# Sums of squares by accumulating transfers, two re-ordered preparation lists, earlier table loads and a pooling split in one streaming-encoder block

## The chip, the cores and the metric

The program runs on one core of one Trainium2 chip. The metric is device time in microseconds (us) of one execution: the median of several executions is what counts. One execution was also recorded by the hardware profiler, and all rows below come from that one. The engines are PE (TensorE, the matrix engine; PEld is its weight load), DVE (VectorE), ACT (ScalarE), POOL (GpSimd) and SP (SyncE, which issues nearly all transfers).

## What is computed

One layer of an encoder block on 1024 tokens of width 1024, in float32:

```python
h = x + 0.5 * swiglu_ffn(rmsnorm(x, norm_ffn1), ffn1_w_in, ffn1_w_out)      # d_ff 2816
u = rmsnorm(h, norm_mix)
q, k, v, g_ret, p, gates = split(u @ w_in)
ret = retention(rotary(q), rotary(k) / 16, v)                 # 4 heads of 256, chunks of 64
ret = ret * rsqrt(mean(ret * ret) + eps) * silu(g_ret)
pool_out = multiscale_pool(p, pool_w, pool_scale)             # windows 2, 4, 8, 16
gate = sigmoid(gates + gate_bias)
merged = gate[0] * (ret @ w_ret_up) + gate[1] * (pool_out @ w_pool_up)
h = h + merged @ w_out
h = h + 0.5 * swiglu_ffn(rmsnorm(h, norm_ffn2), ffn2_w_in, ffn2_w_out)
return rmsnorm(h, norm_final)
```

with `rmsnorm(x, g) = x * rsqrt(mean(x * x) + eps) * g`.

## The kernel before, in words

Every product is made in three matmuls. An operand is split into a high part (a cast on ACT, L164, or a scaled activate, L168) and a low part (the operand less its high part, on DVE, L165 or L169), and PE adds high·high, high·low and low·high (L184, L185, L186). Large products are cut into quarters and done by Strassen's scheme in Winograd's form: seven products in place of eight, whose operands S1 to S4 (of the weights) and T1 to T4 (of the activations) are sums of quarters made on DVE before they are split. The letters behind a tile's name say which product's bank it is (`wo1b` is one of the banks of `wo1`); `c_wS`, `wo1wS`, `vS1w` are weight operands made of such sums, `n3R`, `n3T`, `mgT`, `ruT` activation operands.

The work runs in this order: first feed-forward part (names `a`, norm `n1`), projections and values with their retention and pooling (norm `n2`; `vS`, `q1`, `t1`, `p3`), the merge (`ru` is `w_ret_up`, `wo` is `w_out`, activations `mg`), the second feed-forward part (names `c`, norm `n3`), the final norm. A queue named `flow` holds small steps that are put in by `flow.add` and taken out while products are issued; when a step is put in decides where its instructions stand. A scheduler then sets the order on each engine, in which each engine runs strictly.

A norm works in two stages. While the activations come into being, `Norm.square` squares each block on ACT (L291) and adds it to one tile, here `n3ssq`, on DVE (L303). Later `Next.stats` sums that tile over its partitions on PE (`n3sum`), takes inverse roots on ACT and DVE, and spreads them over the partitions with two matmuls for each half (`n30b`, `n31b`). ACT's functions come in table sets; where another set is needed, an ACT_TABLE_LOAD stands ahead of the function. Two such loads are called for at the program's start by an activate on a one-column tile `warm` (L216 and, in `rotary_tables`, L1190).

`onto` is a transfer issued by POOL that adds its source to its destination; before, it adds the kept residual to the blocks of `wo`. `out_group` makes the blocks of `h` from `w_out`, `handed` puts in the steps that prepare the next product's T operands (its list `f`, by number: 1, 3, 2, 6, 5). `tl`, `raw`, `t4` and `c2` are rings of buffers of their own. In the merge `gates`' tiles (`pg0` to `pg7`) are loaded into `raw`, where the weights of `ru` are loaded too.

Of the kernel before, what the change touches and what calls it, by code (L numbers as in the profile page):

```python
# [13 lines left out]
AF = mybir.ActivationFunctionType  # L14
# [4 lines left out]
S = 1024  # L19
D = 1024  # L20
KT = D // P
# [69 lines left out]
def block_kernel(ctx: ExitStack, tc, x, x_tok, x_two, vecs, f1_in, f1_out, w_in, w_v, pool_w, w_ret, w_pool, w_o,  # L91
# [188 lines left out]
    class Norm:  # L280


        turns = False

        def __init__(self, name):
            self.name, self.ssq, self.seen = name, None, set()
# [6 lines left out]
        def square(self, mt, tokens, src):  # L293
            if self.ssq is None:
                self.ssq = t4(f"{self.name}ssq")
            dst = self.ssq[:, tokens]
            if tokens.start not in self.seen:
                self.squared(dst, src)
                self.seen.update(range(tokens.start, tokens.stop, HD))
            else:  # L300
                q = c2(f"{self.name}q{mt}_{tokens.start}")[:, : tokens.stop - tokens.start]
                self.squared(q, src)
                tt(dst, dst, q, ADD)  # L303

    class Next(Norm):
# [139 lines left out]
                for i in range(4):  # L445
                    flow.add(lambda f=f, i=i: f(i))

        def stats(self, sums=None, between=(), diagonals=None):
            def roots():
                t = sums if sums is not None else token_sums(self.ssq, range(8), self.name)  # L450
                self.r_tok = inverse_root(t, D, self.name)

            def row(q):
                if not q:
                    self.row = t4(f"{self.name}rb")
                to, b = half(self.row, q), spread(self.r_tok[:, 4 * q : 4 * q + 4], f"{self.name}{q}", diagonals)
                if sums is not None:
                    to, b = in_row(to), in_turns(b)
                copy(to, b)
                if q:  # L460
                    self.rb = self.row

            n = max(0, len(between) - 3)
            flow.add(roots, *between[:n], lambda: row(0), *between[n:], lambda: row(1))
# [722 lines left out]
        flow.until(lambda: stored.issuperset(names))  # L1187

    def rotary_tables():
        act(warm, warm, AF.Sigmoid)  # L1190
        for n, z in (("cos", 0), ("sin", 1)):
            tab[n] = t4(n)
            load(tab[n], rope[z])
            tt(tab[n], tab[n], mix.rms(), MUL)

    def project(kind, n):

        at = {"q": 0, "k": KT, "g": 3 * KT, "p": 4 * KT, "t": 5 * KT}[kind] + 2 * n
        name = f"{kind}{n}"
        pair = {}  # L1200
        scaled = kind in "gpt"

        def dest(which):
            tile, j = which
            if tile not in pair:
                pair[tile] = t4(f"{name}{'AB'[tile]}")
            return half(pair[tile], j)

        def evac(which, in0, in1):
            j, dst = which[1], dest(which)  # L1210
            if in1 is not None:
                tt(dst, in0, in1, ADD)
            elif scaled and mix.rb is not None:
                tt(dst, in0, half(mix.rb, j), MUL)
                return
            else:
                copy(dst, in0)
            if scaled and mix.rb is not None:
                tt(dst, dst, half(mix.rb, j), MUL)
            elif scaled:  # L1220
                flow.add(lambda: tt(dst, dst, half(mix.rms(), j), MUL))

        def rotate(j):

            t = {}

            def a():
                if not tab:
                    rotary_tables()
                t["b"], t["c"] = c2(f"{name}b{j}"), c2(f"{name}c{j}")  # L1230
                t["A"], t["B"] = (half(pair[z], j) for z in range(2))
                t["cos"], t["sin"] = half(tab["cos"], j), half(tab["sin"], j)
                tt(t["b"], t["B"], t["sin"], MUL)
                tt(t["c"], t["A"], t["sin"], MUL)

            def b():
                tt(t["A"], t["A"], t["cos"], MUL)
                tt(t["A"], t["A"], t["b"], SUB)

            def c():  # L1240
                tt(t["B"], t["B"], t["cos"], MUL)
                tt(t["B"], t["B"], t["c"], ADD)

            return a, b, c

        def keep(dst):
            for i in range(2):
                load(dst[2 * n + i], pair[i])
            stored.add(name)

        def swish(i):
            act(pair[i], pair[i], AF.Silu)
            load(gs[2 * n + i], pair[i])
            if i:
                stored.add(name)

        def gate(i):
            mt = 2 * n + i
            for j in range(2):
                z = c2(f"{name}z{i}{j}")  # L1260
                act(in_row(z), in_turns(half(pair[i], j)), AF.Sigmoid, bias=vec[:, V_B0 + mt : V_B0 + mt + 1])
                load(half(gates[mt], j), z)
            if i:
                stored.add(name)

        def window(i):

            win = 2 << n
            t = {}

            def double(step):
                s = t.get("s", pair[i])
                o = t["s"] = t4(f"{name}s{i}_{step}")
                tt(o[:, step:], s[:, step:], s[:, : S - step], ADD)
                copy(o[:, :step], s[:, :step])

            def mean():
                z, s = pair[i], t["s"]

                edge = sb.tile([P, 16], F32, tag="edge", bufs=2, name=f"{name}e{i}")  # L1280
                tt(edge, s[:, :16], cst[:, C_CNT + 16 * n : C_CNT + 16 * n + 16], MUL)
                tt(edge, edge, z[:, :16], SUB)
                stt(s, s, 1.0 / win, z, MUL, SUB)
                copy(s[:, :16], edge)
                load(pooled[2 * n + i], s)
                if i:
                    stored.add(name)

            return *(lambda b=b: double(1 << b) for b in range(n + 1)), mean

        def end():
            if kind in "qk":
                turn = (*rotate(0), *rotate(1)) if n < NH - 1 or kind == "k" else ()
                flow.add(*turn, lambda: keep(qs if kind == "q" else ks))
            elif kind == "p":
                flow.add(*window(0), *window(1))
            else:
                f = swish if kind == "g" else gate
                flow.add(lambda: f(0), lambda: f(1))

        return lambda shared: strassen(mix, w_in[at], w_in[at + 1], name, evac, end, shared=shared, dest=dest)

    def values():
# [70 lines left out]
        def result(o, j, other=None):  # L1374
            def after(i, b):
                c = c2(f"vc{o}{j}{i}")
                if other is None:
                    copy(c, b)
                else:
                    tt(c, b, other(i), ADD)  # L1380
                flow.add(lambda: store(o, j, i, c))
                if (o, j, i) == (0, 0, 3):
                    nx.stats(between=nx.blocks("R22", [("tl", N_TL)] * 3, True))

            return after

# [14 lines left out]
        s2, s1 = product("S2", "T2", "a", False, after6), product("S1", "T1", "b", True, after5)  # L1401
        nx.work(nx.t3)
        for k in range(4):
            if k == 2:
                nx.work(nx.r21, nx.t4_)
            yield (lambda a=s2[k], b=s1[k]: (a[0](), b[0]())), s1[k][1]
            yield (lambda: None), s2[k][1]
        for p in zip(product("S4", "R22", "b", False, result(0, 1, lambda i: old("h", i))),
                     product("S3", "T3", "a", False, result(1, 1, lambda i: old("f", i)))):
            yield from p  # L1410
# [60 lines left out]
    def pool_up():  # L1471
        gate, stores = {}, {}
        for mt in range(KT):

            def begin(mt=mt):
                await_stored(f"t{(KT + mt) // 2}")
                if mt < KT - 1:
                    r = raw(f"pg{mt}")
                    load(r, gates[KT + mt])
                    gate[mt] = [half(r, j) for j in range(2)]  # L1480
                    stores[mt] = [(pm[mt], r)]
                    return
# [368 lines left out]

        return [group(n, i) for n, i in enumerate(at)]

    waiting = []

    def out_group(i):
        pair = [None, None]
# [29 lines left out]
    def handed(nx, last):  # L1887
# [3 lines left out]
        def between(pair, n):  # L1891
            if n in (3, 5):
                flow.add(*waiting)
                waiting.clear()
            if pair == 0:
                if n == BY_OPERAND[-1]:
                    flow.add(*(lambda m=m, i=i: m(i) for i in range(2) for m in (nx.r22, nx.sum1, nx.sum3)))
# [2 lines left out]

            for m in {3: (0,), 6: (4,)}.get(n, ()):
                flow.add(*(lambda i=i: f[m](i) for i in range(2, 4)))
            if n == BY_OPERAND[-1]:
                rest = [lambda m=m, i=i: f[m](i) for m in (1, 3, 2, 6, 5) for i in range(2, 4)]
                last(rest)

        return between

    def merge():
        yield from two_by_two(two_groups(0) + two_groups(1), BY_OPERAND, handed(mg, lambda rest: flow.add(*rest)))  # L1910
        yield from two_by_two((out_group(i) for i in range(4)), BY_OPERAND,
                              handed(ffn2, lambda rest: (flow.add(*rest[:4]), ffn2.stats(between=rest[4:]))))

    ffn2 = Next("n3", V_FFN2, h2)
    ops2 = spill("r2", FH), spill("t2", FH), spill("b2", FH), spill("m2", FH, H)

    class Last(Norm):
# [193 lines left out]
```

## Time and profile before

| | |
|---|---|
| median of 3 executions | 2062.12 us (2061.41 to 2063.96) |
| the profiled execution | 2062.72 us, of which its span is 2060.9 us |
| granted TensorE clock | 0.999 of the higher level (2.4 GHz) over the span |
| PE busy | 2040.5 us (99%), 10672 matmuls |
| DVE busy | 1831.2 us (89%) |
| ACT busy | 1092.5 us (53%) |

The span runs from the first to the last instruction on the core; what the execution takes beside it is 1.8 us. A busy share is a mean over a program with many stages; an engine that is not the bound of a stage may wait there at no cost.

### The profile page before, as it was taken

The numbers are of one execution on the slowest core, as the hardware profiler recorded it, in microseconds if no ns is written. First come the engines' busy times: TensorE is split into PE (matmuls) and PEld (weight loads), VectorE is DVE, ScalarE is ACT, GpSimd is POOL, SyncE is SP. The second block draws the span as 40 slices with busy tenths as digits, with TensorE's granted clock in tenths as the row PEclk, the third lists the DMA queues.
The fourth block names the chain that finished last, engine by engine and source line by source line (L and its number), as shares of the span: only waits on it lengthen the run. The fifth ranks groups of instructions, "written<-read, shape, count | busy, mean of one in ns | idle before, by whom it ended". The sixth has DMA issues, their size and how long they took to land.

```text
span 2060.9 us, 29728 instructions
## 1 busy us (share of the span) xinstructions
PE 2040.5 (99%) x10672; PEld 1810.4 (88%) x10672; DVE 1831.2 (89%) x3253; ACT 1092.5 (53%) x2066; POOL 9.1 (0%) x14
## 2 busy tenths in 40 slices
PE   9999999999999999999999999999999999999998
PEld 7888999988888888888888999888889989998887
DVE  8889998998996798989789987899989989899896
ACT  8545454554754554454447753456645545455454
POOL 0000000000000000000000000010000000000000
PEclk9999999999999999999999999999999999999999
DMA  6332424585543333243337667545223232368642
GB/s 245 137 103 77 143 88 143 199 274 196 187 146 109 107 136 110 85 151 119 117 125 229 203 227 278 185 109 163 82 98 133 88 133 88 135 208 274 211 148 97
DMA packets 120260, 313.57 MB, mean 152 GB/s; under 512 B 13361, under 2 KB 17585, under 8 KB 120113
## 3 DMA queue, kind: packets, MB, share of 16 engines
q1 hardware_dynamic: 118096, 308.01, 43.9%
q0 software_dynamic: 1440, 2.62, 0.8%
q8 instruction: 83, 1.36, 0.3%
q10 hardware_dynamic: 576, 1.05, 0.1%
q14 instruction: 65, 0.52, 0.1%
HBM read 220.93 MB, written 90.70 MB: 151 GB/s over the span
## 4 chain that ended last, share of the span: by engine, by line
PE 81%; DVE 12%; DMA 2%; ACT 2%; issue 2%; SPq 0%; ACTq 0%; DVEq 0%
PE c_b L185 2%; PE c_b L184 2%; PE c_b L186 2%; PE a_b L184 2%; PE a_b L186 2%; PE a_b L185 2%; PE c_e L186 2%; PE c_e L184 2%; PE c_e L185 2%; PE a_e L186 1%; PE a_e L184 1%; PE a_e L185 1%; PE a_a L186 1%; PE a_a L185 1%; PE a_a L184 1%
## 5 line engine op out<-in xcount | busy, mean ns | idle before, releaser
L184 PE MATMUL c_b<-n3T,c_wS 128*128 128x512 f32 x176 | 66.8, 380 | 1.7 <-ACT n3T L164 1.7
L185 PE MATMUL c_b<-n3T,c_wS 128*128 128x512 f32 x176 | 66.8, 380 | 0.0
L186 PE MATMUL c_b<-n3T,c_wS 128*128 128x512 f32 x176 | 66.7, 379 | 0.0
L184 PE MATMUL a_b<-n1T,a_wS 128*128 128x512 f32 x168 | 63.7, 379 | 0.0
L185 PE MATMUL a_b<-n1T,a_wS 128*128 128x512 f32 x168 | 63.7, 379 | 0.0
L186 PE MATMUL a_b<-n1T,a_wS 128*128 128x512 f32 x168 | 63.7, 379 | 0.0
L184 PE MATMUL a_a<-n1R,a_wL 128*128 128x512 f32 x120 | 45.5, 379 | 0.0
L186 PE MATMUL a_a<-n1R,a_wL 128*128 128x512 f32 x120 | 45.5, 379 | 0.0
L185 PE MATMUL a_a<-n1R,a_wL 128*128 128x512 f32 x120 | 45.5, 379 | 0.0
L184 PE MATMUL c_a<-n3R,c_wL 128*128 128x512 f32 x112 | 42.7, 381 | 0.7 <-ACT c_b L529 0.5
L185 PE MATMUL c_a<-n3R,c_wL 128*128 128x512 f32 x112 | 42.4, 379 | 0.0
L186 PE MATMUL c_a<-n3R,c_wL 128*128 128x512 f32 x112 | 42.4, 379 | 0.0
L184 PEld LDWEIGHTS c_b<-n3T,c_wS 128*128 128x128 f32 x176 | 33.3, 189 | 6.6 <-ACT n3T L164 2.1
L185 PEld LDWEIGHTS c_b<-n3T,c_wS 128*128 128x128 f32 x176 | 33.3, 189 | 4.8 <-DVE n3T L165 0.3
L186 PEld LDWEIGHTS c_b<-n3T,c_wS 128*128 128x128 f32 x176 | 33.3, 189 | 4.7
L186 PEld LDWEIGHTS a_b<-n1T,a_wS 128*128 128x128 f32 x168 | 31.8, 189 | 4.5
L185 PEld LDWEIGHTS a_b<-n1T,a_wS 128*128 128x128 f32 x168 | 31.8, 189 | 4.4
L184 PEld LDWEIGHTS a_b<-n1T,a_wS 128*128 128x128 f32 x168 | 31.8, 189 | 4.4
L165 DVE TENSOR_TENSOR a_wS<-a_S,a_wS 128x512 fp32r<-128x512 f32 x45 | 30.7, 684 | 3.8 <-ACT a_wS L164 3.8
L165 DVE TENSOR_TENSOR c_wS<-c_S,c_wS 128x512 fp32r<-128x512 f32 x46 | 31.2, 681 | 2.6 <-ACT c_wS L164 2.6
L164 ACT CAST a_wS<-a_S 128x512 fp32r<-128x512 f32 x45 | 27.3, 621 | 11.7 <-PE a_a L186 6.1
L184 PE MATMUL c_e<-n3T,c_wS 128*128 128x512 f32 x88 | 33.5, 380 | 0.0
(3167 smaller groups left out, 8012.2 us busy)
## 6 DMA issues: line engine op xcount, KB each, us to landing
c_ra<-in_f_in SPq DMA_DIRECT2D x22, 512.0 KB, 3.6
c_rb<-in_f_in SPq DMA_DIRECT2D x22, 512.0 KB, 3.5
a_ra<-in_f_in SPq DMA_DIRECT2D x21, 512.0 KB, 3.7
a_rb<-in_f_in SPq DMA_DIRECT2D x21, 512.0 KB, 3.7
t<-au SPq DMA_DIRECT2D x11, 512.0 KB, 3.5
b<-ag SPq DMA_DIRECT2D x11, 512.0 KB, 4.1
r<-au SPq DMA_DIRECT2D x11, 512.0 KB, 3.7
bra<-in_f_out SPq DMA_DIRECT2D x11, 512.0 KB, 5.5
```

The lines of the kernel that those rows point to most:

```text
L164: copy(hi, src)
L165: tt(lo, src, hi.bitcast(F32), SUB)
L184: mm(dst, w[0], m[0], start=start, stop=False, skip_group_check=True)
L185: mm(dst, w[0], m[1], start=False, stop=False, skip_group_check=True)
L186: mm(dst, w[1], m[0], start=False, stop=stop, skip_group_check=True)
```

## The change

Six edits. `Norm` gets an attribute `aside`. For the second feed-forward part's norm it is `apart`: a square that is not the first of its column range is put into half a `tl` tile, and is added to `n3ssq` either by an accumulating transfer (`onto`) or, for the others, by a DVE addition that waits in the list `sums` until `settled` puts all of them in. `handed` puts the steps of a pair's last product in another order (1 and 3 of one block, then 5, then 2, 6, 5), and no longer puts in steps 0 and 4 of blocks 2 and 3 elsewhere. `stats` gets an activate on `warm` with the function that is needed next, behind the roots; the one in `rotary_tables` goes. One gates' tile (`pg6`) is loaded into the ring `tl`. In the values, steps `r21` and `t4_` are put in behind the loop. In the pooling of the widest window (n is 3) each doubling is done in two halves.

```diff
+            elif self.aside:
+                self.aside(mt, tokens, dst, src)
             else:
                 q = c2(f"{self.name}q{mt}_{tokens.start}")[:, : tokens.stop - tokens.start]
...
-        def stats(self, sums=None, between=(), diagonals=None):
+        def stats(self, sums=None, between=(), diagonals=None, then=AF.Silu):
             def roots():
                 t = sums if sums is not None else token_sums(self.ssq, range(8), self.name)
                 self.r_tok = inverse_root(t, D, self.name)
+                act(warm, warm, then)
...
     def rotary_tables():
-        act(warm, warm, AF.Sigmoid)
...
-                tt(o[:, step:], s[:, step:], s[:, : S - step], ADD)
+                ends = (step, H, S) if n == 3 else (step, S)
+                for a, z in zip(ends, ends[1:]):
+                    tt(o[:, a:z], s[:, a:z], s[:, a - step : z - step], ADD)
...
-                    nx.stats(between=nx.blocks("R22", [("tl", N_TL)] * 3, True))
+                    nx.stats(between=nx.blocks("R22", [("tl", N_TL)] * 3, True), then=AF.Sigmoid)
...
         for k in range(4):
-            if k == 2:
-                nx.work(nx.r21, nx.t4_)
             yield (lambda a=s2[k], b=s1[k]: (a[0](), b[0]())), s1[k][1]
             yield (lambda: None), s2[k][1]
+        nx.work(nx.r21, nx.t4_)
...
-                    r = raw(f"pg{mt}")
+                    r = (tl if mt == KT - 2 else raw)(f"pg{mt}")
...
-    waiting = []
+    waiting, sums, spare = [], [], []
+
+    def apart(mt, tokens, dst, src):
+
+        if not spare:
+            q = tl(f"n3q{mt}_{tokens.start}")
+            spare.extend((half(q, 1), half(q, 0)))
+        q = spare.pop()
+        ffn2.squared(q, src)
+        if mt % 4 < 2 or mt < 4 and not tokens.start:
+            onto(dst, q)
+        else:
+            sums.append(lambda: tt(dst, dst, q, ADD))
...
+            if pair and n == BY_OPERAND[-1]:
+                rest = [lambda m=m, i=i: f[m](i) for m, at in ((1, 2), (3, 2), (5, 0), (2, 2), (6, 2), (5, 2))
+                        for i in (at, at + 1)]
+                last(rest)
+                return
...
-            if n == BY_OPERAND[-1]:
-                rest = [lambda m=m, i=i: f[m](i) for m in (1, 3, 2, 6, 5) for i in range(2, 4)]
-                last(rest)
-
         return between
+
+    def settled(rest):
+
+        flow.add(*rest[:4], lambda: [f() for f in sums[:3]], lambda: [f() for f in sums[3:]])
+        ffn2.stats(between=rest[4:])
...
-                              handed(ffn2, lambda rest: (flow.add(*rest[:4]), ffn2.stats(between=rest[4:]))))
+                              handed(ffn2, settled))
```

The edits move instructions on the engines at many places; three of them follow. The first is the start of the program on ACT, as a difference (a minus is a row of before, a plus one of the changed kernel; `a_w` and `n1R` are the first operands that PE waits for).

```order
-L1190 ACT_TABLE_LOAD
-L1190 ACTIVATE warm<-warm 128x1
+L454 ACT_TABLE_LOAD
+L454 ACTIVATE warm<-warm 128x1
+L454 ACT_TABLE_LOAD
+L454 ACTIVATE warm<-warm 128x1
 L164 CAST a_w_296<-ra 128x512
 L168 ACTIVATE n1R_310<-x_92,vec 128x512
+L454 ACT_TABLE_LOAD
+L454 ACTIVATE warm<-warm 128x1
 L168 ACTIVATE n1R_316<-x_93,vec 128x512
 L168 ACTIVATE n1R_322<-x_94,vec 128x512
```

The activates on `warm` hang on nothing but each other, and stand at the start and not behind the roots: three table loads with their activates where one was. The loads that stand at the functions' first uses (L241, L796 and others before; L241, L799 and others now) are in the listing as before, so that the program has twelve loads where it had ten.

The second place is ACT in the first pair of `wo` products. Before:

```order
L164 CAST wo1wS_13683<-wo1S_13681 128x512
L164 CAST mgT_13706<-ru_13292 128x512
L164 CAST mgT_13710<-ru_13328 128x512
L1876 COPY wo_13686<-wo1a 128x512
L164 CAST mgT_13731<-mgt_13667 128x512
L164 CAST mgT_13734<-mgt_13673 128x512
L291 ACTIVATE n3ssq<-wo_13648 128x512
L164 CAST wo0wS_13714<-wo0rb 128x512
L534 COPY wo0v<-wo0b 128x512
L164 CAST wo1wS_13738<-wo1rb 128x512
```

The changed kernel, same engine and place:

```order
L164 CAST mgT_13740<-mgt_13644 128x512
L164 CAST mgT_13743<-mgt_13650 128x512
L1891 COPY wo_13697<-wo1a 128x512
L164 CAST wo1wS_13694<-wo1S_13692 128x512
L164 CAST wo0wS_13723<-wo0rb 128x512
L291 ACTIVATE n3ssq<-wo_13663 128x512
L537 COPY wo0v<-wo0b 128x512
L291 ACTIVATE n3q_0_13852<-wo_13697 128x512
L164 CAST wo1wS_13747<-wo1rb 128x512
```

The first `wo1wS` cast has moved behind the `mgT` casts, and a square (`n3q_0_13852`, of a block that an accumulating transfer has to reach first) now stands ahead of the second `wo1wS` cast.

The third place is DVE where the second feed-forward part begins. Before:

```order
L165 TENSOR_TENSOR c_wS_14312<-c_S_14310,c_wS_14312 128x512
L492 TENSOR_TENSOR c_S_14336<-c_S_14334,c_ra 128x512
L505 TENSOR_TENSOR c_rb<-c_ra,c_rb 128x512
L303 TENSOR_TENSOR n3ssq<-n3ssq,n3q_512_14385 128x512
L165 TENSOR_TENSOR c_wS_14338<-c_S_14336,c_wS_14338 128x512
L303 TENSOR_TENSOR n3ssq<-n3ssq,n3q_512_14407 128x512
L165 TENSOR_TENSOR n3R_14427<-wo_13650,n3R_14427 128x512
L165 TENSOR_TENSOR c_wS_14361<-c_rb,c_wS_14361 128x512
L303 TENSOR_TENSOR n3ssq<-n3ssq,n3q_512_14420 128x512
L165 TENSOR_TENSOR n3R_14430<-wo_13688,n3R_14430 128x512
L303 TENSOR_TENSOR n3ssq<-n3ssq,n3q_512_14424 128x512
L165 TENSOR_TENSOR c_wS_14389<-c_rb,c_wS_14389 128x512
```

The changed kernel, same engine and place:

```order
L165 TENSOR_TENSOR c_wS_14314<-c_S_14312,c_wS_14314 128x512
L355 SCALAR_TENSOR_TENSOR wo_13992<-n3t_14424,neg,wo_13994 128x512
L361 TENSOR_TENSOR n3t_14434<-wo_14021 128x512
L355 SCALAR_TENSOR_TENSOR wo_13992<-wo_13992,neg,wo_13994 128x512
L165 TENSOR_TENSOR n3T_14427<-wo_13992,n3T_14427 128x512
L165 TENSOR_TENSOR c_wS_14340<-c_S_14338,c_wS_14340 128x512
L355 SCALAR_TENSOR_TENSOR wo_14021<-n3t_14434,neg,wo_14023 128x512
L355 SCALAR_TENSOR_TENSOR wo_14021<-wo_14021,neg,wo_14023 128x512
L1869 TENSOR_TENSOR n3ssq<-n3ssq,n3q_512_14387 128x512
L165 TENSOR_TENSOR c_wS_14363<-c_rb,c_wS_14363 128x512
L165 TENSOR_TENSOR n3T_14437<-wo_14021,n3T_14437 128x512
```

The sums `c_S` and the two differences (L355, L353 before) that make `n3T` stand earlier against the weights, and the additions to `n3ssq` no longer stand between them.

## Rows read from the trace of the kernel before

**Rows 1.** The page, part 1: busy time, share of the span and instructions of each engine.

```profile
PE 2040.5 (99%) x10672; PEld 1810.4 (88%) x10672; DVE 1831.2 (89%) x3253; ACT 1092.5 (53%) x2066; POOL 9.1 (0%) x14
```

**Rows 2.** PE's waits: engine, tile, line, who released it; total, times, longest.

```profile
PE ru1a L184 <- ACT ru1b L529: 1.8, 1, 1.8
PE c_b L184 <- ACT n3T L164: 1.7, 1, 1.7
PE wo2a L184 <- ACT wo2b L529: 1.3, 1, 1.3
...
PE q1b L184 <- DVE q1B L1212: 0.6, 1, 0.6
...
PE c_a L184 <- ACT c_b L529: 0.5, 1, 0.5
PE vS L185 <- DVE vS1w L165: 0.5, 1, 0.5
```

**Rows 3.** ACT, timeline 0 to 8 us: start, duration, line, operation, repeats [idle before].

```profile
0.74 1.28 ACT L216 ACT_TABLE_LOAD   x1 [0.74 <-PEq L2100]
2.03 0.20 ACT L216 ACTIVATE warm<-warm 128x1 f32<-128x1 f32 x1
2.25 1.28 ACT L1190 ACT_TABLE_LOAD   x1
...
4.09 0.62 ACT L164 CAST a_w<-ra 128x512 fp32r<-128x512 f32 x1 [0.34 <-DMA ra<-in_f_in]
5.44 1.35 ACT L168 ACTIVATE n1R<-x,vec 128x512 fp32r<-128x512 f32 x2 [0.74 <-DMA x<-in_x]
7.27 1.33 ACT L168 ACTIVATE n1R<-x,vec 128x512 fp32r<-128x512 f32 x2 [0.48 <-DMA x<-in_x]
```

**Rows 4.** PE, timeline, the ninth matmul on real data.

```profile
9.16 0.38 PE L186 MATMUL a<-n1R,a_w 128*128 128x512 f32 x1
```

**Rows 5.** DVE, timeline 624 to 631 us (values).

```profile
624.43 0.69 DVE L165 TENSOR_TENSOR vS1w<-vS,vS1w 128x512 fp32r<-128x512 f32 x1
...
629.98 0.69 DVE L165 TENSOR_TENSOR vS1w<-vS,vS1w 128x512 fp32r<-128x512 f32 x1
```

**Rows 6.** PE, timeline, the values' second wait.

```profile
630.72 0.48 PE L185 MATMUL vS<-vS1w,n2T 128*128 128x512 f32 x1
```

**Rows 7.** DVE, timeline, the widest pooling's last doubling.

```profile
851.94 1.21 DVE L1274 TENSOR_TENSOR p3s<-p3s 128x1016 f32<-128x1016 f32 x1
```

**Rows 8.** ACT, timeline 1304 to 1312 us (`ru`).

```profile
1309.18 0.62 ACT L164 CAST ruT<-ret 128x512 fp32r<-128x512 f32 x1 [4.73 <-DVE ret L390]
1309.71 0.58 ACT L529 COPY ru1b<-ru1a 128x512 f32<-128x512 f32 x1
```

**Rows 9.** DVE, groups by line: the additions of squares (busy, mean ns | idle before).

```profile
L303 DVE TENSOR_TENSOR n3ssq<-n3ssq,n3q 128x512 f32<-128x512 f32 x14 | 9.6, 686 | 2.6 <-ACT n3q L291 2.6
```

**Rows 10.** Transfers issued in 1384 to 1394 us: KB each, median us to landing.

```profile
wo<-h POOLq DMA_DIRECT2D x2, 256.0 KB, 4.3
```

**Rows 11.** POOL, timeline, the issue of the second of them.

```profile
1388.77 0.86 POOL L143 DMA_DIRECT2D wo<-h  x1 [2.74 <-ACT wo L1876]
```

**Rows 12.** ACT, timeline, the first `wo1wS` of the S2·T2 product.

```profile
1386.16 0.62 ACT L164 CAST wo1wS<-wo1S 128x512 fp32r<-128x512 f32 x1 [1.36 <-DVE wo1S L492]
```

**Rows 13.** PE, timeline, the first matmul that reads it.

```profile
1388.14 0.38 PE L184 MATMUL wo1b<-mgT,wo1wS 128*128 128x512 f32 x1
```

**Rows 14.** DVE, timeline, an addition of squares where the second feed-forward part begins.

```profile
1451.27 0.68 DVE L303 TENSOR_TENSOR n3ssq<-n3ssq,n3q 128x512 f32<-128x512 f32 x1
```

**Rows 15.** ACT, timeline 1454 to 1456 us.

```profile
1454.53 0.62 ACT L164 CAST c_wS<-c_S 128x512 fp32r<-128x512 f32 x1 [2.25 <-DVE c_S L492]
1455.05 0.58 ACT L529 COPY c_b<-c_a 128x512 f32<-128x512 f32 x1
```

**Rows 16.** DVE, timeline, the first step behind `n3sum`.

```profile
1473.15 0.17 DVE L240 TENSOR_SCALAR n3v<-n3sum 128x8 f32<-128x8 f32 x1 [0.97 <-PE n3sum L254]
```

**Rows 17.** PE, timeline, the first spread of the roots.

```profile
1480.82 0.63 PE L277 MATMUL n30b<-n30dg,ones_r 128*128 128x512 f32 x2
```

More of the change, by code (lines that the diff above doesn't have):

```diff
@@ L280, in block_kernel @@
     class Norm:
-        turns = False
+        turns, aside = False, None
         def __init__(self, name):
@@ L1911, in merge @@
         yield from two_by_two((out_group(i) for i in range(4)), BY_OPERAND,
-                              handed(ffn2, lambda rest: (flow.add(*rest[:4]), ffn2.stats(between=rest[4:]))))
+                              handed(ffn2, settled))
     ffn2 = Next("n3", V_FFN2, h2)
+    ffn2.aside = apart
     ops2 = spill("r2", FH), spill("t2", FH), spill("b2", FH), spill("m2", FH, H)
```

## The prediction, made before the changed kernel was run

> **What bounds the kernel now.** I read the page first: PE is busy 2040.5 of 2060.9 us [rows 1], so all that any edit can give back lies in PE's idle 20 us, and any wait that an edit adds on PE's path is paid in full. DVE at 89% has little room, ACT at 53% has much, but both run in order, and one late row holds up those behind it. Then I read the list of what PE waits for [rows 2]: the waits are few, short and each at one place, so the change is a matter of six places. At each I read the timelines of DVE and ACT, laid the order of the changed kernel over them with the same durations, and asked when the operand that PE wants is ready. Times of the changed kernel below are such estimates, made from rows; each place is taken by itself, then summed.
>
> **The function loads.** The listing shows that the loads do not move behind the roots: they stand at the program's start, two more of them, and those at first use remain. So the edit removes nothing from the later program and adds two loads with their activates. One pair takes from 0.74 to 2.25, that is 1.51 us [rows 3]. Two come ahead of the first cast `a_w`: one stood there before, so it is later by one pair, less the 0.34 us that ACT waited there for a transfer: 4.09 becomes about 5.25. `n1R` then starts at about 5.8 where it was 5.44, because 0.74 us of waiting for `x` takes up most of the delay. The third load stands behind that first `n1R`, and there is nothing to hide it: the second `n1R` (half of the x2 row, so at about 6.1 before) starts at about 8.0, the third at about 8.6 in place of 7.27, since 0.48 us of waiting went. PE needs each of them in turn with its low part from DVE behind it; its ninth matmul, at 9.16 [rows 4], comes at about 10.5. From there on PE has operands in stock. I take **+1.4 us**; the bounds are +1.1 (the delay of the third `n1R`, less some idle time that PE had in any case) and +1.9 (that of the second).
>
> The trace has one pair following another at 1.51 us, with nothing between. The Trainium skill (ScalarE: Activation LUTs, section What ACT_TABLE_LOAD costs) gives 1283 ns for the load, which agrees with the row's 1.28, but puts a drain of some 1380 ns to each switch, 2.66 us in all. By that rule the two loads would cost 5.3 us on ACT, not 3.0, and this term would be about 3.7.
>
> **The values.** With `r21` and `t4_` put in behind the loop, the weights' `vS1w` for the loop's last two rounds come ahead of the `n2R` and `bacc` steps on DVE. PE waits 0.5 us for the `vS1w` whose low part starts at 624.43 [rows 2, 5], and again for the one that starts at 629.98 and ends at 630.67, since its reader starts at 630.72 [rows 5, 6]. The first comes about a quarter of a us earlier, the second is no longer late: **−0.6 us** (−0.85 if the first vanishes by half, −0.2 if its ring slot holds it). The moved steps have products in front of them, so nothing is late in their place.
>
> **The pooling.** One doubling over 1016 columns takes 1.21 us [rows 7]; two halves take about 0.68 each, the second overlapped by 0.08, so DVE pays some 0.06 us more each time, about half a us over eight of them. A half lets another step in between. PE waits 0.6 us for `q1B` [rows 2], which stands just behind such a doubling; it may be ready half a us earlier, but in the new order PE comes to it earlier by about as much. **0** (−0.5 to +0.5).
>
> **The gates' tile.** With `pg6` out of `raw` the weights of `ru` are loaded sooner, by some ten us. The 1.8 us that PE loses at `ru1a` [rows 2] are not due to these loads, though: the copy `ru1b` at 1309.71 stands on ACT behind a cast `ruT` that waited 4.73 us for DVE [rows 8]. In the new order two such casts stand ahead of the copy, each with a DVE step to wait for, and DVE, which saves the wait for weights, reaches the second of them about when it reached the first. **−0.1 us** (−0.6 to +0.9).
>
> **The merge.** Squares: 14 additions at 0.69 us leave 9.6 us on DVE [rows 9]; eight go to transfers, some 4.8 us at the 0.60 at which they follow each other. They gain time only where PE waits. At `wo1b` the new order costs: the first `wo1wS` cast started at 1386.16 [rows 12] and is ready with its low part 0.3 us ahead of PE's need at 1388.14 [rows 13]. Now two more DVE steps and the `mgT` casts stand ahead; the cast starts at about 1389, its low part ends at about 1390.2, and PE loses some 1.5 us. A shorter wait behind it, under half a us, then goes, and the wait of 1.3 us at `wo2a` [rows 2] goes as well, since `wo2S` no longer queues behind additions of squares. In between ACT stands at the square `n3q`, for which the transfer issued at 1388.77 [rows 11] must have landed, 4.3 us later at 1393.1 [rows 10]; behind it are the casts of the second `wo1wS`, ready at about 1395.2 where PE comes at 1395.5. Sum of this stretch **−0.3 us** (−1.7 if the first `wo1wS` is in time, +1.0 if the landing bites).
>
> **The second feed-forward part's start.** PE waits here three times: 0.5 for the copy `c_b`, 1.7 for `n3T` [rows 2], and a shorter one, with restarts about 3.2 us. Both operands stand in line on DVE behind additions like that at 1451.27 [rows 14], and the copy at 1455.05 stands on ACT behind a cast for which ACT waited 2.25 us [rows 15]. In the new order the sums `c_S` are made before `wo` is done, and `n3T`'s differences come ahead of the additions: I get the copy done at about 1453.9, where PE wants it at 1454.7, and the late `n3T` 1.5 us ahead of its reader. **−3.2 us** (−3.4 to −1.5, the latter if one of the two waits stays because ACT's copies stand behind the scaling of `wo`, which waits for the store of `wo`).
>
> What is late next: `n3sum` moves 18 matmuls towards `n30b`, so PE leaves only 3.9 us (18 at 0.216) between them. Before, the chain from `n3v` at 1473.15 to `n30b` at 1480.82 had 7.7 us [rows 16, 17], but other DVE steps of 0.6 us filled it; in the new order the small steps follow each other, and I count about 3.5 us. **+0.1 us** (0 to +4).
>
> Sum: 1.4 − 0.6 + 0 − 0.1 − 0.3 − 3.2 + 0.1 = −2.7 us. The profiled execution took 2062.72, which is 0.6 above the median of 2062.12; as a median the forecast is 2062.12 − 2.7 = **2059.4 us**.
>
> **The rivals.**
> 1. *No wait at `wo1b`.* If the first `wo1wS` is in time, all of the squares' waits go: −4.1 in all, 2058.0, and lower with the values' and the gates' bounds, to about 2056.5. For it: DVE has 4.8 us less to do here. Against it: the order above, in which the cast stands behind four others.
> 2. *Half of the gain at `c`.* One wait stays: 2061.1. For it: ACT's copy still stands behind rows that wait for DVE and for stores.
> 3. *Slower: the roots are late.* If the chain from `n3sum` to `n30b` takes the 7.7 us that it took before, PE stands for about 3.8 us more, and the sum is +1.0: 2063.1; with the loads' +1.9 and half of the gain at `c`, 2065.3. It decides from the point where the chain is longer than 6.6 us, since the gain of 2.7 is then eaten up. For it: the chain crosses engines six times. Against it: nothing long stands between its steps now.
> 4. *The change doesn't do what it says.* For the loads I already hold this. If the transfers' additions were to hold up POOL's later ones (`h`'s blocks), the squares' gain would go: about 2062.5.
>
> A rival that the Trainium skill's drain makes: each load stalls ACT for that long too. As a mechanism here, the two added pairs would be 2.3 us longer and the forecast 2061.7. The rows, with 2.25 less 2.03 for the whole activate, speak against it.
>
> **How the numbers follow.** Chances: the forecast 0.42, rival 1 0.24, rival 2 0.15, rival 3 0.11, rival 4 0.05, the drain 0.03. The range from 2055.5 to 2063.5 takes in rival 1 with its lower bounds and rivals 2 and 4; most of rival 3 and more than is reckoned on either side is left out. About 0.2% (4.1 us) is what a measurement of this kernel can tell from no change. Faster by more than that, so under 2058.0, is most of rival 1 and the forecast's lower edge: 0.32. Slower than 2066.2 needs rival 3 with bad bounds elsewhere, or a wait that I don't see: 0.08. Within: 0.60.
>
> **What would show it.** In the changed profile: four table loads ahead of PE's tenth matmul, and that matmul 1.4 us later; the `vS` wait at 0.25; `ru1a` still at about 1.8; a new wait of about 1.5 at `wo1b`; no waits at `wo2a`, `c_a` and `c_b`; `n30b` with no wait over 0.3. The prediction is wrong if waits come up at places that the list of before does not have, first of all in the `wo` products, or if `c_b` still waits for `n3T`.

## The result, and the profile after

The changed kernel takes 2072.61 us (median of 6 executions, 2070.62 to 2076.09), the kernel before 2063.64 us on the same chips (6 executions). The ratio is 1.0047, with a 95% interval from 1.0037 to 1.0058: slower by some 9 us. The profiled execution has a span of 2071.2 us, 10.3 more than before.

PE's waits in the changed kernel (engine, tile, line, who released it; total, times, longest):

```profile
PE c_a L184 <- ACT c_b L532: 4.6, 1, 4.6
PE wo1e L184 <- ACT wo1wS L164: 1.4, 1, 1.4
...
PE a L184 <- ACT n1R L168: 0.9, 2, 0.6
PE ru1a L184 <- ACT ru1b L532: 0.9, 1, 0.9
PE vS L185 <- DVE vS1w L165: 0.8, 1, 0.8
...
PE wo1b L184 <- ACT wo1wS L164: 0.6, 1, 0.6
...
PE wo1b L186 <- DVE wo1wS L165: 0.4, 1, 0.4
```

Against [rows 2] the wait for `n3T` and the one at `wo2a` are gone, as forecast, and `wo1b` is there, as forecast; but the wait for the copy `c_b` has grown from 0.5 to 4.6 us where it was to vanish, and `wo1e` is new. Laying the start of each matmul beside that of the same matmul before (its shift is the difference) shows how the 10.3 us come together: 2.7 by 13 us of the program, 1.4 more spread over 257 to 458 us, next to nothing on balance between 644 and 1378, 1.7 at `wo1b`, 0.5 back at `wo0e`, 1.9 at `wo1e`, 1.2 back at `wo2a`, 0.7 in small steps up to `c_a`, 4.1 at `c_a`, and 0.8 less behind it, where the wait for `n3T` is saved and the lower clock is paid. The last 0.5 come in tenths behind 1600.

The start, on ACT, timeline 0 to 8 us:

```profile
2.25 1.28 ACT L454 ACT_TABLE_LOAD   x1
...
3.76 1.28 ACT L454 ACT_TABLE_LOAD   x1
...
5.17 0.60 ACT L164 CAST a_w<-ra 128x512 fp32r<-128x512 f32 x1
5.67 0.72 ACT L168 ACTIVATE n1R<-x,vec 128x512 fp32r<-128x512 f32 x1
6.41 1.28 ACT L454 ACT_TABLE_LOAD   x1
...
7.81 1.32 ACT L168 ACTIVATE n1R<-x,vec 128x512 fp32r<-128x512 f32 x2
```

The third `n1R`, at 7.27 before [rows 3], is the second half of the last row here. PE's answer, by stretches of time (busy time of each engine with its instructions, then granted clock, share of DMA, GB/s):

```profile
5.00:10.00 5.00, 3.47 (x10) 1.52 (x9) 2.83 (x5) 4.96 (x10) 0.00 (x0) 0.91 1.02 347
10.00:12.20 2.20, 2.20 (x7) 1.73 (x6) 2.20 (x4) 2.20 (x5) 0.00 (x0) 0.50 1.01 372
1461.00:1466.50 5.50, 0.89 (x5) 0.46 (x4) 5.50 (x10) 5.50 (x11) 0.00 (x0) 1.00 0.25 95
1466.50:1469.50 3.00, 3.00 (x8) 2.37 (x9) 2.86 (x6) 2.61 (x6) 0.00 (x0) 0.51 0.00 0
```

Behind the waits at 6 to 9 us, and again behind the 4.6 us at `c_a`, the granted clock stands at 0.50 and 0.51, so at the lower level, 1.2 GHz: PE does its matmuls 0.43 us apart where they were 0.216. This costs some 1.5 us at the start (2.7 in all, of which runs e2 and e4 below lose 1.2 with the clock up) and 1.3 us behind `c_a` (the shift grows from 10.65 to 11.94), on top of the waits.

How the copy `c_b` came to be late shows in the chain that led up to it (in order of time: start, us, what):

```profile
1429.75 1.14 POOL wo L143
1430.88 3.40 issue
1434.30 4.61 DMA wo<-h
...
1439.58 1.32 ACT n3R L168 x2
...
1443.49 0.63 ACT wo3wL L164
...
1444.14 0.70 DVE wo3wL L165
...
1444.86 4.72 DMA c_rb<-in_f_in
...
1450.29 0.68 DVE wo L1889
...
1455.09 0.69 DVE wo L1897
...
1455.81 0.76 ACT n3q L291
...
1465.80 0.49 ACT c_b L532
...
1466.33 0.59 PE c_a L184
```

The fourth of the six transfers that add the residual to blocks of `wo` is issued at 1434.30, some 1.8 us later than PE's shift of 6.2 alone would put it: its copy (L1891, at 1433.32) now stands on ACT behind two `n3T` casts that wait for DVE, where before it stood ahead of them. The transfer lands at 1438.9; a square stands for it at the head of ACT's queue; the casts behind the square free the weights' buffers late; so `c_rb` is loaded late; DVE waits for `c_rb` with a sum `c_S`, which now stands ahead of the row that makes the next block of `wo` (L1889); and behind that block ACT stands again for its square. The rows of ACT that waited, and that copy:

```profile
1399.20 0.74 ACT L291 ACTIVATE n3q<-wo 128x512 f32<-128x512 f32 x1 [4.58 <-DMA wo<-h]
...
1431.52 0.62 ACT L164 CAST n3T<-wo 128x512 fp32r<-128x512 f32 x1 [2.03 <-DVE wo L355]
...
1433.32 0.58 ACT L1891 COPY wo<-wo3a 128x512 f32<-128x512 f32 x1
...
1438.93 0.75 ACT L291 ACTIVATE n3q<-wo 128x512 f32<-128x512 f32 x1 [1.26 <-DMA wo<-h]
...
1455.81 0.75 ACT L291 ACTIVATE n3q<-wo 128x512 f32<-128x512 f32 x1 [6.79 <-DVE wo L1897]
...
1465.71 0.57 ACT L532 COPY c_b<-c_a 128x512 f32<-128x512 f32 x1
```

and of DVE:

```profile
1449.68 0.69 DVE L495 TENSOR_TENSOR c_S<-c_rb 128x512 f32<-128x512 f32 x1 [1.11 <-DMA c_rb<-in_f_in]
1450.29 0.68 DVE L1889 TENSOR_TENSOR wo<-wo2b,wo2p 128x512 f32<-128x512 f32 x1
```

Before, the block's row stood ahead of the first `c_S`, 4.3 us sooner when PE's shift is taken off. The two rows:

```profile
1439.82 0.68 DVE L1874 TENSOR_TENSOR wo<-wo2b,wo2p 128x512 f32<-128x512 f32 x1
...
1451.87 0.68 DVE L492 TENSOR_TENSOR c_S<-c_rb 128x512 f32<-128x512 f32 x1
```

and ACT's square behind that block:

```profile
1446.00 0.75 ACT L291 ACTIVATE n3q<-wo 128x512 f32<-128x512 f32 x1 [3.14 <-DVE wo L1882]
```

The order on ACT behind that square has changed as well: the copy `c_b` stood ahead of the last four squares and the two scalings of `wo` (L346) and now stands behind them (L348 now), so from the square to the copy it is 9.9 us with 1.4 us of waiting in it (1455.81 to 1465.71), where it was 9.1 with 3.8 us of waiting (1446.00 to 1455.05 [rows 15]).

The first wait, 4.58 us, is what makes the wait at `wo1e`. POOL had issued the transfer at 1392.82:

```profile
1392.82 0.86 POOL L143 DMA_DIRECT2D wo<-h  x1 [3.26 <-ACT wo L1891]
```

so it took 6.4 us to the square's start at 1399.20, where [rows 10] had 4.3.

### The profile page after: what moved, and what is told of

The parts are those of the page before. It is cut to its first block, busy times and chain, and to the rows that moved or that the text cites. A ratio compares the mean times of both kernels' runs of the same rounds, so it can differ in the third digit from the quotient of the medians.

```text
span 2071.2 us, 29761 instructions
## 1 busy us (share of the span) xinstructions
PE 2046.6 (99%) x10672; PEld 1813.5 (88%) x10672; DVE 1827.8 (88%) x3253; ACT 1095.0 (53%) x2070; POOL 16.1 (1%) x22
## 5 line engine op out<-in xcount | busy, mean ns | idle before, releaser
L799 ACT ACTIVATE ag<-ag 128x1024 f32<-128x1024 f32 x22 | 23.3, 1058 | 20.0 <-DVE ag L791 15.5
```

The source lines that it names most:

```text
L799: flow.add(scale, lambda: act(gate, gate, AF.Silu), lambda: times(0), lambda: times(1))
```

## The experiments

Theory: the squares put apart (edit of `Norm`, `apart`, `settled`) make the loss in `wo` and `c`, because the scheduler now sets them early on ACT, where they stand for landings; the loads make the loss at the start. Rivals: the new order in `handed`; the accumulating transfers by themselves; chance orders elsewhere. Medians are over all executions of a run's kernel; the kernel before, run beside them, had 2062.18 (first four), 2062.05 (next four) and 2062.26 us (last four).

**e1_undo_loads**

```diff
-                act(warm, warm, then)
...
     def rotary_tables():
+        act(warm, warm, AF.Sigmoid)
```

> The changed kernel with the function loads of before (no activate behind the roots, the one in rotary_tables back), all else changed. Theory: the two loads at the start cost 2.7 us, of which 1.4 us are waits of PE for n1R and 1.3 us are six matmuls that then run at the lower clock (0.43 us apart in place of 0.216), and the extra waits at a_x near 272, 309 and 345 us (1.2 us in all) come from another order that the loads bring about, so 2072.6 falls to about 2069 (span 2067.3) and the PE rows at 10 us stand 0.216 apart. Rival: only the waits hang on the loads and the clock falls at the start by itself; then 1.4 us are gained, 2071.2, with rows at 0.43 still there.

Measured: 2068.44 us, ratio 1.0034 (1.0021 to 1.0047). At 13 us of the program the shift against before is 0.1 in place of 2.7, and it is 0.4 at 458 us in place of 4.1. The time agrees with the theory's 2069, and the start with its 2.7 us. What is lost at `a_x` between 257 and 458 us, 1.4 in the changed kernel, is 0.3 to 1.0 in the other profiles with the loads, so this part varies and is not settled. The profiled execution took 2071.59 us, 3.2 above the median, so places are read from it and not the time.

**e2_undo_squares**

```diff
-    ffn2.aside = apart
...
-        flow.add(*rest[:4], lambda: [f() for f in sums[:3]], lambda: [f() for f in sums[3:]])
+        flow.add(*rest[:4])
```

> The changed kernel with the squares of the second feed-forward norm added at once by DVE, as before; the new order of the last product's steps stays. Theory: the wait of 4.6 us at c_a for the copy c_b, with the 1.3 us of low clock behind it, comes from the squares put apart, since ACT stands at them until the accumulating transfers have landed; so the c_a wait falls under 1 us, the wo1e wait of 1.4 us goes, and the time falls by 6 to 8 us to about 2065.5. Rival: the order of the steps (sums c_S ahead of the DVE row that starts the transfers of wo) makes the wait; then c_a still loses over 3 us and the time stays above 2069.

Measured: 2064.57 us, ratio 1.0014 (1.0005 to 1.0023). The waits at `wo1e` and at `c_a` beyond 0.5 us are gone:

```profile
PE c_b L184 <- ACT n3T L164: 1.0, 1, 1.0
PE wo2a L184 <- ACT wo2b L532: 1.0, 1, 1.0
...
PE wo1b L184 <- ACT wo1wS L164: 0.6, 1, 0.6
PE c_a L184 <- ACT c_b L532: 0.5, 1, 0.5
```

The waits at `wo1b` stay, with the new order in `handed`. The theory holds for `wo1e` and `c_a`, and the rival falls; whether the landings or something else in the squares' edit makes the loss, this run doesn't tell.

**e3_undo_handed**

```diff
-            if pair and n == BY_OPERAND[-1]:
-                rest = [lambda m=m, i=i: f[m](i) for m, at in ((1, 2), (3, 2), (5, 0), (2, 2), (6, 2), (5, 2))
-                        for i in (at, at + 1)]
-                last(rest)
-                return
...
+            if n == BY_OPERAND[-1]:
+                rest = [lambda m=m, i=i: f[m](i) for m in (1, 3, 2, 6, 5) for i in range(2, 4)]
+                last(rest)
```

> The changed kernel with the order of the steps in handed as before; the squares stay apart. Theory (squares): the wait at c_a stays over 3 us, only the waits of 1.0 us at wo1b go, and the time is about 2071. Rival (order): c_a's wait falls under 1 us and the time falls to about 2066.

Measured: 2071.58 us, ratio 1.0049 (1.0034 to 1.0064). The wait at `c_a` is 4.5 us with the old order too, and `wo1b` doesn't wait, so the theory holds:

```profile
PE c_a L184 <- ACT c_b L532: 4.5, 1, 4.5
```

**e4_only_loads**: the kernel before, with the edit that e1 undoes.

> The kernel before with the edit of the function loads alone. Theory: +2.7 us at the start, of which 1.3 by the clock, and up to +1.2 more at a_x: 2063.6 becomes 2066.3 to 2067.5. Rival (waits alone, no clock): +1.4, 2065.

Measured: 2064.63 us, ratio 1.0013 (1.0004 to 1.0023), so 2.5 us for the edit alone; taken out of the changed kernel (e1) it is worth 4.2 in the medians. In the profile the start loses 1.2 us here, with the same gaps of PE as the changed kernel has up to 9.4 us, but the clock stays up:

```profile
10.00:12.20 2.20, 2.20 (x12) 1.90 (x11) 2.20 (x4) 2.20 (x5) 0.00 (x0) 1.00 1.05 401
```

Of the seven profiles with the loads (the changed kernel, e2 to e7), five show the lower clock here and two (e2, e4) don't. So the theory's 2.7 is the sum of waits of about 1.2 that come each time and of 1.5 that come with the clock; the latter isn't certain, and the rival (waits alone) has this profile right. With the loads of before no profile shows the lower clock here. Only 0.4 us came at `a_x`.

**e5_ring_alone**

```diff
         ffn2.squared(q, src)
-        if mt % 4 < 2 or mt < 4 and not tokens.start:
-            onto(dst, q)
-        else:
-            sums.append(lambda: tt(dst, dst, q, ADD))
+        tt(dst, dst, q, ADD)
```

> The changed kernel in which every square is added at once by DVE, so with no accumulating transfer and no late sum, but still put into the ring tl and not into c2. Theory (ring): what harms is that n3q no longer takes buffers of the ring c2, since then the sums c_S of the next part get buffers sooner and stand ahead on DVE of the row that starts the transfers of wo; so c_a still waits over 3 us and the time is about 2070. Rival (transfers): the accumulating transfers and the waits for them harm; then c_a's wait is under 1 us and the time is about 2065.

Measured: 2068.72 us, ratio 1.0032 (1.0022 to 1.0042), so slow with no accumulating transfer of squares at all. The waits:

```profile
PE c_a L184 <- ACT c_b L532: 1.6, 1, 1.6
PE wo2a L184 <- ACT wo2b L532: 1.4, 1, 1.4
PE wo3a L184 <- ACT wo3b L532: 1.3, 1, 1.3
...
PE wo1e L184 <- ACT wo1wS L164: 1.2, 1, 1.2
```

The theory's time is near; its "over 3 us at `c_a`" is wrong, since PE comes there later. Behind `c_a` the granted clock stays at 1.00 here:

```profile
1466.00:1470.00 4.00, 3.86 (x18) 3.41 (x19) 4.00 (x8) 3.15 (x7) 0.00 (x0) 1.00 0.00 0
```

This kernel and e2 differ in the ring alone, so the ring alone costs 4.2 us (2068.72 against 2064.57); the changed kernel is another 3.9 us slower than this one.

**e6_c2_transfers**

```diff
-        if not spare:
-            q = tl(f"n3q{mt}_{tokens.start}")
-            spare.extend((half(q, 1), half(q, 0)))
-        q = spare.pop()
+        q = c2(f"n3q{mt}_{tokens.start}")
...
-            sums.append(lambda: tt(dst, dst, q, ADD))
+            tt(dst, dst, q, ADD)
```

> The changed kernel with the eight accumulating transfers, but the squares in the ring c2 as before and the other six added at once. Theory (ring): c_a's wait is under 1 us, the wo1e wait of 1.4 us goes, and the time is about 2064.5, as without the squares edit. Rival (transfers): c_a's wait stays over 3 us, and the time is about 2071.

Measured: 2064.06 us, ratio 1.0008 (0.9999 to 1.0018). No wait at `wo1e`, and 1.8 us at `c_a` where the theory had under 1. From the start of `wo` to the restart at `c_a` the copy comes 0.9 us later than before; with `tl` (changed kernel) 6.7 us, with `tl` and no transfers (e5) 5.7. So from `c2` the transfers do no harm (e6 is no slower than e2), and the ring does harm without them (e5). It isn't the ring alone, though: the 3.9 us between e5 and the changed kernel come where the eight transfers and the six late additions are put on top of the ring `tl`, and no run has one of these two without the other there. What they change is seen in the order on ACT: the copy of `wo3a` stands behind the two `n3T` casts in the changed kernel, e1, e3, e7 and e10, which have all three, and ahead of them in every other profile. The profiled execution of e6 took 2067.73 us, 3.7 above the median, and e12, with the same squares and order, has no wait at `c_a`, so the 1.8 us here are no firm price.

What the ring does is seen in the rows: `c2` (8 buffers) also holds the sums `c_S`. With the squares in `c2` (before, e2, e6, e8, e11, e12) the row of DVE that makes `wo`'s block from `wo2b` stands ahead of the first `c_S` of the next part (1442.39 and 1456.52 us in this run), and the copy `c_b` ahead of the last four squares; with the squares in `tl` (the changed kernel, e1, e3, e5, e7, e10) the block stands behind two or three `c_S`, the copy behind the squares. In the changed kernel three of them stand ahead, from

```profile
1445.96 0.69 DVE L495 TENSOR_TENSOR c_S<-c_rb 128x512 f32<-128x512 f32 x1
```

to the one at 1449.68 shown above. The squares of ACT stand early in its row, as in the second place shown ahead of the prediction. That the scheduler moves them because they no longer wait for a buffer of `c2` is how I read it; the runs show the order, not its reason.

**e7_no_residual**

```diff
-                onto(dst, half(h1[i + 4 * tile], j))
```

> The changed kernel without the six accumulating transfers that add the kept residual to blocks of wo, so these blocks lack the residual and the output differs. It shows what the waits of ACT's squares for these landings are worth: the theory that ACT stands 4.6 us near 1395 and again near 1434 to 1439 and 1452 to 1456 for landings has the waits at wo1e gone and c_a's wait 2 to 4 us shorter, span about 2065; if the order of DVE alone makes it (c_S behind a late weight load), c_a's wait stays at 4 us or more, span above 2068.

Measured: one execution, 2066.89 us, span 2065.1. No wait at `wo1e`; the copy comes 0.6 us later than before from the start of `wo`, in place of 6.7, and `c_a` waits 1.5:

```profile
PE c_a L184 <- ACT c_b L532: 1.5, 1, 1.5
```

The early `c_S` rows are still there, with 0.6 us of waiting for `c_rb`. So the order on DVE is not enough: the long wait needs the residual's transfers, for whose landing ACT's squares stand. Its time understates this, since this profile is 3.5 us slower by the start of `wo` (at 1378) than at 700, at places that the edit doesn't touch. By stretches, from 1378 to 1500 us of before, it gains 1.9 us, where the changed kernel loses 5.9, e10 5.7, e5 3.2, and e2 and e6 0.9 each. Both theories of the landing and of the ring are needed together.

**e8_values_c2**: the kernel before, with the values' edit and the `apart` of e6 alone.

> The kernel before with two edits alone: the values' steps later, and the eight accumulating transfers of squares from the ring c2. Theory: values give 0.6 us (seen between 464 and 631 us where the loads' edit is in), the transfers save 4.8 us of DVE and up to 1.5 us at wo2a and c_b: 2062.2 falls to 2060.0 to 2061.5. Rival: the transfers' saving meets no wait, 2061.6; or their landings bite, over 2063.

Measured: 2060.16 us, ratio 0.9990 (0.9981 to 0.9999): within 0.2%, but faster by more than its measurement is uncertain. `vS` waits 0.3 and `wo2a` 0.2 us:

```profile
PE vS L185 <- DVE vS1w L165: 0.3, 1, 0.3
PE wo2a L184 <- ACT wo2b L531: 0.2, 1, 0.2
```

**e9_values**: the values' edit alone.

> The kernel before with the values' edit alone. Theory: the waits at vS shrink by 0.6 us and nothing else moves, so 2062.1 becomes 2061.5, and what the kernel with values and transfers gained beyond it (2060.2) is the transfers'. Rival: the whole gain of 1.9 us is the values' and chance order behind them: 2060.2 here too.

Measured: 2062.28 us, ratio 1.0000 (0.9991 to 1.0009). In the profile the stretch from 623 to 644 us gains 0.5, as the theory has it; the time doesn't show it. The medians of e8 and e9 are 2.1 us apart, which would be the transfers' share, but their intervals overlap; the profiles place 0.7 of it (from 1378 to 1500 us e8 gains 0.8, e9 0.1).

**e10_squares**: the squares' edit alone.

> The kernel before with the squares' edit alone (ring tl, eight transfers, six late additions). Theory (squares from tl stand early on ACT and wait there for the residual's transfers): +1.3 us at wo1e, the copy c_b 5 to 7 us later against the stage's start, 1 us more from the lower clock behind the long wait, 1 to 2 us given back at c_b: 2062.1 becomes about 2068. Rival: it needs the new order of handed or the late start too; then under 2064.

Measured: 2069.55 us, ratio 1.0032 (1.0020 to 1.0044). `wo1e` costs 1.4 us (0.8 of it the wait itself) and the copy `c_b` comes 6.5 us later, as in the changed kernel; no other edit is needed. Alone, the squares cost 7.3 us and the loads 2.5 (e4), together about what the whole change costs.

```profile
PE c_a L184 <- ACT c_b L531: 4.5, 1, 4.5
```

**e11_small_c2**: e8 with the gates' tile and the pooling in halves.

> The kernel before with values, gates' tile, pooling in halves, and the transfers of squares from c2; no loads, no new order in handed. Theory: gates and pooling are worth nothing within 0.5 us, so about 2060.2, as with values and transfers alone. Rival: the gates' tile takes 1 us off the wait at ru1a: 2059.2.

Measured: 2060.41 us, ratio 0.9992 (0.9983 to 1.0000): both edits together are worth nothing that can be told, as the theory has it. `ru1a` waits 1.2 us here. In the nine profiles with the gates' edit it waits 0.6 to 2.0 us; in the five without it, 1.8 (before), 0.3 (e4) and nothing (e8, e9, e10). So the edit doesn't take this wait away, and may add to it; the time shows neither.

**e12_c2_noloads**: the changed kernel with the loads of before and the squares as in e6.

> The changed kernel with the loads of before and the squares in c2 (transfers kept, the other six added at once). Theory: what is left against the kernel before is 1.65 us lost at wo1b by the new order, about 1.5 us won back at wo0e and wo2a, and 0.6 us of the values: 2061 to 2062, with PE at 10 us as before. Rival: the new order in handed harms in the next part too: over 2063.

Measured: 2061.37 us, ratio 0.9996 (0.9986 to 1.0005), as forecast: with the loads and the ring undone the change is no slower than before. In the profile 1.7 us go at `wo1b` and 2.1 come back at `wo0e` and `wo2a`.

## Why the prediction was wrong

It said 2059.4 us and gave a slower kernel by over 0.2% a chance of 0.08; 2072.6 was measured. The terms:

- **Loads, +1.4.** The reason was right, they stand at the start. The waits were 1.2 (e2, e4), and 1.3 to 1.7 more came with the clock, in five of seven profiles, which the prediction hadn't reckoned with: its upper bound of 1.9 holds no change of clock. In the medians the edit cost 2.5 (e4) and 4.2 (e1). The drain of 1380 ns that the Trainium skill (ScalarE: Activation LUTs, section What ACT_TABLE_LOAD costs) puts to a switch is not to be seen: the loads follow each other from 2.25 to 3.76 us, 1.51 apart as before, and the third starts at 6.41, right behind the `n1R` that ends at 6.39.
- **Values, −0.6.** Between 623 and 644 us 0.5 to 0.6 were gained in eight profiles (e2, e3, e5 to e9, e11), 0.2 in two (e1, e12), nothing in the changed kernel's, where `vS` waited 0.8. In the time it can't be told (e9).
- **Pooling, gates: 0 and −0.1.** Agree in the time (e11), for what can be told. The reason given for the gates, that `ru1a` would wait about as before, isn't borne out one way or the other: 0.9 us in the changed kernel, 0.6 to 2.0 in all with the edit.
- **Merge, −0.3.** It measured +2.7 (the shift goes from 3.9 at 1378 us of before to 6.6 just ahead of `c_a`), outside its bound of +1.0. Three parts of it were right: 1.7 us at `wo1b` (1.5 forecast), the wait of `wo0e` gone, that of `wo2a` gone (e6, e12). What failed is the sentence that ACT stands at `n3q` until 1393.1 and that the casts behind it just fit: 1.9 us were paid at `wo1e`. The issue at 1392.82 is where it was to be (1388.77 [rows 11] and the shift of 3.9), but the square started 6.4 us behind it, not 4.3. This is not a chance spread: the second residual transfer took 6.2 to 6.5 us in all six profiles that have it with the new order in `handed` (the changed kernel, e1, e2, e5, e6, e12), and 4.5 to 4.7 in the seven with the old. A duration taken from the old order was laid on the new one. In e10, where PE isn't held up at `wo1b`, 4.7 us are enough to cost 1.4 as well, so 0.3 us of slack was too little either way.
- **Second feed-forward part, −3.2.** This is the step that made the prediction wrong: it measured +3.2 (the shift goes from 6.6 at 1455 us of before to 9.8 at 1492). "I get the copy done at about 1453.9" took the times at which `wo`'s blocks are made from the trace of before, and laid the new order on ACT and DVE over them. But in the new order the block is itself later by 4.3 us (its row on DVE at 1450.29, at 1439.82 before, with 6.2 us of shift by then), through the loop of copy, landing, square, weight cast, load, `c_S`, block that the chain shows. The replay saw each place by itself; the loop runs through ACT, POOL, the load queue and DVE and starts 30 us ahead of the wait. A second part of the step failed on ACT alone: where that row of DVE is late by 0.2 us (e5) or 0.8 (e7) alone, PE still loses 1.0 us at `c_a`, with the copy behind four squares and two scalings. The bound of −1.5 named the scalings, but as a wait that stays, not as one that grows. And no term had the lower clock behind a long wait, 1.3 us here.
- **Roots, +0.1.** Right: `n30b` doesn't wait, though the last `n3sum` now starts 4.1 us ahead of it in place of 8.0.

Of the rivals the slower one (the late roots) had another mechanism and did not happen. The fourth, that POOL's later transfers are held up by the squares', did not happen as written either: the fifth residual transfer was late, but POOL stood idle for 8.3 us until DVE had made its block, so it was not the squares' transfers ahead of it that held it up:

```profile
1451.38 0.87 POOL L143 DMA_DIRECT2D wo<-h  x1 [8.26 <-DVE wo L1889]
```

The loss was also far more than the 2062.5 written there. What the prediction named as a sign of being wrong, waits at places that the list of before does not have, first in the `wo` products, is what came.

What stays open: how the 6.4 and 4.6 us from issue to landing split into the transfer's own time and other traffic beside it, and why the new order in `handed` makes the first of them longer; and which of the eight transfers and the six late additions, put on the ring `tl`, sets the `n3T` casts ahead of the copy of `wo3a`. That the clock falls at the start in some executions and not in others at the same gaps of PE isn't explained.

## What to carry to other kernels

A buffer ring can hold back the order as well as the space. Moving fourteen squares here from a ring of eight buffers to another changed the order on ACT and DVE with nothing else altered (e5 against e2, 4.2 us): work of the next part stood early, ahead of rows that other engines waited for; so a move of a tile is to be read from the order of all engines that use both rings, not from the engine that it saves.

A row that must wait for a transfer costs what stands behind it on its engine, so a replay of a new order has to carry each delay around its loop, through POOL, the landing, the loads that wait for a freed buffer and back, before it says that a wait vanishes.

An activate with no operand but its own tile is not held to the place where it is written: here it went to the start, and was paid there.

## What the runs showed of the hardware

PE's granted clock fell to 0.50 behind short gaps at the start (five of seven profiles with the same gaps) and to 0.51 behind one gap of 4.6 us, while before the change, with gaps up to the 1.8 us at `ru1a`, its mean over the whole span was 0.999. Behind the 1.6 us at `c_a` in e5 it stayed at 1.00. An accumulating transfer of 256 KB issued by POOL took 3.2 to 6.4 us from issue to landing in the changed kernel (18 of them) and 3.8 to 4.5 before (10 of them). The Trainium skill (DMA: Bandwidth & Descriptors, section Anatomy of one DMA — SWDGE (gpsimd) path) fits a transfer of that path with 2.0 us and the bytes over 436 GB/s, by estimate 2.6 us for this size; the measured landings are all longer.
